# Differential heads: two pairs' norm products in one bank, posted behind the first scores

## The chip, the cores and the metric

The kernel runs on one core of a Trainium2 chip. The metric is device time in microseconds (us), the median of several runs. The core has a matrix engine (TensorE; PE in the profile, with its weight loads shown as PEld), a vector engine (DVE), a scalar engine (ACT), GpSimd (POOL), and a queue that issues the DMA transfers (SP). Products land in banks of PSUM, from which DVE and ACT read them; POOL works on SBUF only.

## The reference

A two-layer encoder over 1024 tokens of width 1024. Layer 0 has windowed, dense and memory cross attention; layer 1 has six differential heads and four cross-attention heads. Each layer ends in a gate, an output projection and the residual. What the change touches is layer 1's differential attention:

```python
def blk(args):                          # one block of 128 queries
    n, qi = args
    s = jnp.einsum("ibqhd,ibshd->ibhqs", qi, kk).astype(jnp.float32) * (D ** -0.5)
    ...
    p = jax.nn.softmax(s + rel_bias_lookup(table, rel)[None, None], axis=-1)
    w = p[0] - lam * p[1]
    return jnp.einsum("bhqs,bshe->bqhe", w.astype(v.dtype), v)
...
y_c = diff_attention_blocked(...)
y_c = rmsnorm(y_c, subln_g) * (1.0 - lam_init)
y = jnp.concatenate([y_c.reshape(Bn, S, -1), ...], axis=-1) * jax.nn.silu(gate)
return x + y @ w_out
```

The RMS norm of `y_c` runs over the 128 values that one head gives for one token. Its two small matrix products and what hangs on them are what moves.

## The kernel before, in words

**Steps.** Layer 1's attention is a list of 56 steps: 8 for cross attention, then 6 heads of 8 query blocks each, one block of 128 queries to a step. Two blocks (an even and an odd one) make a pair, and there are 24 pairs. `run_steps` (line 441) walks through the steps and posts, for step i, in this order: the DMA that copies the weights `e` of step i-1 (`hop`); the scores of step i (`s1`); some of the pending projection work (`jobs.pull`); whatever earlier pairs have left in `posts`; for the pair whose second block lies three steps back, the product with the values (`s3`, whose list of follow-up functions goes to `posts`); the transposes of the step two back (`s2`); the rest of step i's softmax (`finish`); and some more projection work.

**One differential step.** `s1` (line 1420) makes eight score matmuls: four with the high part of the keys (line 1433) and four with the low part (line 1439), which use 64 rows of the array each. I call the last four the kl scores. DVE adds the bias and takes the minimum (line 1445), ACT exponentiates (line 1448), DVE combines the two maps (line 1457). The result is copied by DMA and transposed two steps later, in eight transposes of 128x128 (line 540, tile `te`), four to a bank; ACT and DVE split each bank into a high and a low part (lines 315 and 316).

**One pair.** In the even step, `s3` multiplies the values by the transposed weights, 24 matmuls (line 1472, tile `oc`). ACT copies the result to `O` and squares it to `sq`. The norm follows in two posts. `d1`, in the step after: two products of `sq` with a column of ones (line 1487, tile `ssqc`; the profile shows each as two matmuls), ACT adds the epsilon term (line 1491, tile `z`), and POOL takes the power (line 229, tile `rz`). `d2`, one step later again: two transposes that spread the result over the partitions (line 1500, tile `rbcc`), DVE scales `O` (line 1502), POOL multiplies it into the gate tile (line 1505), and behind the last pair of a head the tile is stored (`store_y`).

**Banks.** `ps_t` (line 218) hands out banks of tag T, of which there are two. In layer 1's heads `te` takes two of them a step, `ssqc` and `rbcc` one each, and the transposes of the values (`tv`, line 405) one for each half of a head's values.

**Projection work.** `jobs.pull(n)` posts n groups of eight matmuls of 128x512 (line 297), which project the next heads' queries, keys, values and gates. In a differential step two groups come behind the scores and one at the end. When all projections are done, early parts of the output product (line 662, tile `pre`) come from the same place, one group behind the scores.

**Order.** The program's order gives each instruction its rank. The tool that builds the kernel plans the order on each engine from the ranks, from estimated durations and from the free buffers, so instructions of one engine can change places where a bank or an input is not there in the plan. `tc.issue_after` ties a few of them to another instruction.

Of the kernel before, what the change touches and what calls it, by code (L numbers as in the profile page):

```python
# [14 lines left out]
AF = mybir.ActivationFunctionType  # L15
# [3 lines left out]
P = 128  # L19
# [136 lines left out]
def encoder_kernel(ctx, tc, A):  # L156
    nc = tc.nc
# [23 lines left out]
    ones2 = const.tile([P, 2], F32, name="ones2")  # L181
# [36 lines left out]
    def ps_t(name):  # L218
        return ps.tile([P, 512], F32, tag="T", name=name, bufs=2)

    def ps_a(name):
        return ps.tile([P, 512], F32, tag="A", name=name, bufs=2)

    def stat(name, n=1, bufs=3):
        return sm.tile([P, n], F32, tag=name, name=name, bufs=bufs)

    def rstd_from(dst, var, n):
        nh = nhalf[:, :n] if isinstance(n, int) else nhalf[:, :n[0] * n[1]].rearrange("p (a b) -> p a b", b=n[1])
        return nc.gpsimd.tensor_tensor(out=dst, in0=var, in1=nh, op=ALU.pow)  # L229
# [83 lines left out]
    def split_to(hi, lo, src, scale=None):  # L313
        if scale is None:
            nc.scalar.copy(hi, src)  # L315
            return nc.vector.tensor_tensor(out=lo, in0=src, in1=hi, op=ALU.subtract)  # L316
        else:
            nc.scalar.activation(hi, src, AF.Identity, scale=scale)  # L318
            return nc.vector.scalar_tensor_tensor(out=lo, in0=src, scalar=scale, in1=hi,
                                           op0=ALU.mult, op1=ALU.subtract)  # L320
# [17 lines left out]
    def transpose_tile(xt, hT, t):  # L338
        hh, hl = hT
        for j in range(2):  # L340
            T = ps_t("tx")
            for i in range(4):
                k = 4 * j + i
                nc.tensor.transpose(T[:, i * P:(i + 1) * P], xt[:, k * P:(k + 1) * P], ident)
            o = slice(t * P, (t + 1) * P)
            Tv = T.rearrange("p (k c) -> p k c", k=4)
            split_to(hh[:, 4 * j:4 * j + 4, o], hl[:, 4 * j:4 * j + 4, o], Tv)
# [50 lines left out]
    def v_consume(M, c0, n, acc, put):  # L398
# [3 lines left out]
        def d():  # L402
            T = ps_t("tv")
            for i in range(n // P):
                nc.tensor.transpose(T[:, i * P:(i + 1) * P], raw[:, i * P:(i + 1) * P], ident)
            put(c0 // P, n // P, T)
# [34 lines left out]
    def run_steps(steps, jobs, hooks=None, pace=None):  # L441
        n = len(steps)
        posts = deque()
        p2 = p3 = 0
        finish = None
        for i in range(n + LAG + 1):
            behind = None
            if jobs is not None:
                jobs.step = i
            if hooks:  # L450
                hooks(i)
            if 0 < i <= n and steps[i - 1].hop:
                steps[i - 1].hop()
            if i < n:
                if steps[i].need:
                    jobs.ensure(*steps[i].need)
                finish = steps[i].s1()
            f = steps[min(i, n - 1)].fill
            if jobs is not None:
                if half[0] and len(wout) >= 8 and jobs.projected():  # L460
                    f = pace(i)
                two = f > 1 and p3 < n and p3 + steps[p3].lag + 1 <= i and steps[p3].s3b is not None
                jobs.pull(f - f // 2 - two)
                if hooks:
                    hooks(-1)
            for q in list(posts):
                q.pop(0)()
                if not q:
                    posts.remove(q)
            if p3 < n and p3 + steps[p3].lag + 1 <= i:  # L470
                st, p3 = steps[p3], p3 + 1
                if st.s3 is not None:
                    if st.need3:
                        jobs.ensure(*st.need3)
                    r = st.s3()
                    if r:
                        posts.append(r)
                    if st.s3b is not None:
                        jobs.pull(two)
                        st.s3b()  # L480
            if p2 < n and p2 + steps[p2].lag <= i:
                behind = steps[p2].s2()
                p2 += 1
            if finish:
                with (tc.issue_after(behind.ins) if behind is not None else nullcontext()):
                    finish()
                finish = None
            if jobs is not None:
                jobs.pull(f // 2)
                if hooks:  # L490
                    hooks(-1)
        while posts:
            for q in list(posts):
                q.pop(0)()
                if not q:
                    posts.remove(q)
# [170 lines left out]
    def store_y(l, m, g):  # L667
        dma(ysc[l][m], g)
        stored.add((l, m))
# [304 lines left out]
    for k in range(KT):  # L974
        if k % 2 == 0:
            T = ps_t("tm")
# [232 lines left out]
    def hooks0(i):  # L1209
        if 2 <= i < 8:  # L1210
            skew(i - 2)
        if i < 0:
            wout_hook(0, jobs, "g2", r1)

    run_steps(steps, jobs, hooks0, lambda i: i % 4 != 3)
    jobs.drain()
    top_stack.close()
# [176 lines left out]
    jobs = Jobs(jl, ld)  # L1394

    toeps = {}

    def load_toep(h):
        t = M.pl.tile([P, TOEP], F32, tag="toep", name="toep", bufs=2)
        dma(t[:, 768:1152], skew_src(h))  # L1400
        for i in range(2):
            nc.gpsimd.tensor_copy(t[:, 1152 * i:1152 * i + 768], far[:, i, h:h + 1].to_broadcast([P, 768]))
        toeps[h] = t
# [6 lines left out]
    for h in range(6):  # L1410
        for qb in range(8):
# [52 lines left out]
            if st.sub == 1:  # L1464
                def s3(h=h, qb=qb, grp=grp):
                    ph, pl_ = grp["pt"]
                    V = C[h]["v"]
                    acc = ps_a("oc")[:, :256]
                    n = 0
                    for kt in range(8):  # L1470
                        for v, pt in ((0, ph), (0, pl_), (1, ph)):
                            nc.tensor.matmul(acc, V[:, kt, v, :], pt[:, kt, :], start=(n == 0), stop=(n == 23))  # L1472
                            n += 1
                    O = M.pl.tile([P, 256], F32, tag="O", name="O", bufs=2)
                    nc.scalar.copy(O, acc)
                    sq = M.pl.tile([P, 256], F32, tag="sq", name="sqc", bufs=2)
                    nc.scalar.activation(sq, acc, AF.Square)
                    z2 = stat("es", 2)
                    zv = grp["z"].rearrange("p (t m) -> p t m", m=2)[:, :, 0]
                    nc.vector.scalar_tensor_tensor(out=z2, in0=zv, scalar=EPS, in1=zv,  # L1480
                                                   op0=ALU.mult, op1=ALU.mult)
                    st_ = {}

                    def d1():
                        T = ps_t("ssqc")
                        for i in range(2):
                            nc.tensor.matmul(T[:, 2 * i:2 * i + 2], sq[:, i * P:(i + 1) * P], ones2,  # L1487
                                             start=True, stop=True)
                        v = stat("z2", 2)
                        for i in range(2):  # L1490
                            nc.scalar.activation(v[:, i:i + 1], T[:, 2 * i:2 * i + 1], AF.Identity,
                                                 scale=1.0 / 128, bias=z2[:, i:i + 1])
                        r = stat("rz2", 2)
                        rstd_from(r, v, 2)
                        st_["r"] = r

                    def d2():
                        T = ps_t("rbcc")
                        for i in range(2):
                            nc.tensor.transpose(T[:, i * P:(i + 1) * P],  # L1500
                                                st_["r"][:, i:i + 1].to_broadcast([P, P]), ident)
                        nc.vector.scalar_tensor_tensor(out=O, in0=O, scalar=gs, in1=T[:, 0:256],  # L1502
                                                       op0=ALU.mult, op1=ALU.mult)
                        g = gates[h][:, (qb - 1) * P:(qb + 1) * P]
                        nc.gpsimd.tensor_tensor(out=g, in0=O, in1=g, op=ALU.mult)
                        if qb == 7:
                            store_y(1, 2 + h, gates[h])
                    return [d1, d2]
                st.s3 = s3
                st.need3 = ("v%d" % h, "g%d" % h)  # L1510
            st.need = ("k%d" % h, "q%d" % h)
            steps.append(st)
    def hooks1(i):
        if i == 3:
            load_toep(0)
        if i < 0:
            wout_hook(1, jobs, "g5", r2)

    run_steps(steps, jobs, hooks1, lambda i: 2)
    jobs.drain()  # L1520
    left.close()
# [74 lines left out]
```

## Time and profile before

| | |
|---|---|
| Runs | 1242.15, 1242.44, 1243.17 us; median 1242.44 |
| The profiled execution | 1241.79 us; its span, first to last instruction, 1240.0 us |
| Granted TensorE clock, mean | 0.997 |
| Layer 1's differential steps | from about 715 to 1175 us |
| `ssqc` matmuls | 96, from 733.2 to 1170.7 us |
| `rbcc` transposes | 48, from 741.7 to 1172.4 us |

All times in the profile are of one execution, counted from its first instruction. "Busy" is the time in which an engine had an instruction in work. TensorE's matmuls are pipelined, so a recorded length covers more than the time until the next can start; what a group costs is read from start to start. "Idle before" in square brackets names the time for which an engine stood still ahead of an instruction, and what released it.

### The profile page before, as it was taken

How to read it: one execution, taken by the hardware profiler on the slowest of the kernel's cores; microseconds unless marked ns; L12 is line 12 of the kernel's file. 1: busy time of each engine (PE TensorE's matmuls, PEld its weight loads, DVE VectorE, ACT ScalarE, POOL GpSimd, SP SyncE). 2: the span in 40 equal slices, each digit the busy share in tenths (PEclk: the TensorE clock that was granted, in tenths of full speed). 3: DMA queues.
4: the chain of work that ended last, by engine and by line, in shares of the span. 5: the costliest groups of instructions: out<-in, count | busy, mean ns of one | idle time of the engine just before them, and what ended most of it. 6: DMA issues, size and time to landing. Idle time of an engine off the chain costs nothing. (4 is left out here: it accounts for less than half of the span.)

```text
span 1240.0 us, 19680 instructions
## 1 busy us (share of the span) xinstructions
PE 1202.2 (97%) x6806; PEld 999.9 (81%) x6806; DVE 805.7 (65%) x1479; ACT 651.9 (53%) x1453; POOL 412.1 (33%) x390
## 2 busy tenths in 40 slices
PE   5999999999999899999999999999999999999997
PEld 4788888888887788877888788888787878877886
DVE  5547665477777778647356866766767676678544
ACT  6248754367667776533157633544444454456322
POOL 5023365466666655403022221222222121223100
PEclk9999999999999999999999999999999999999999
DMA  6664445545465565376545333242342432546354
GB/s 255 195 194 146 161 170 167 164 159 202 175 229 203 193 236 198 149 211 224 170 151 162 119 111 123 88 143 102 111 134 79 139 112 102 162 141 203 119 197 147
DMA packets 96638, 199.91 MB, mean 161 GB/s; under 512 B 11510, under 2 KB 31222, under 8 KB 96540
## 3 DMA queue, kind: packets, MB, share of 16 engines
q1 hardware_dynamic: 96540, 198.66, 47.7%
q8 instruction: 54, 0.88, 0.3%
q14 instruction: 44, 0.36, 0.1%
HBM read 79.32 MB, written 31.47 MB: 89 GB/s over the span
## 5 line engine op out<-in xcount | busy, mean ns | idle before, releaser
L297 PE MATMUL acc<-h,wh 128*128 128x512 f32 x1536 | 499.2, 398 | 2.1 <-DVE wh L239 0.8
L297 PEld LDWEIGHTS acc<-h,wh 128*128 128x128 f32 x1536 | 283.1, 188 | 66.9 <-issue 12.4
L297 PE MATMUL acc<-h,wl 128*128 128x512 f32 x768 | 304.5, 396 | 1.0 <-POOL wl L241 1.0
L241 POOL TENSOR_TENSOR wl<-wr,wh 128x512 fp32r<-128x512 f32 x96 | 124.4, 1296 | 334.5 <-DVE wh L239 147.2
L316 DVE TENSOR_TENSOR PTl<-te,PTh 128x512 fp32r<-128x512 f32 x224 | 148.3, 686 | 120.9 <-ACT PTh L315 118.3
L1448 ACT ACTIVATE e<-e,mn 128x1024 f32<-128x1024 f32 x96 | 110.1, 1149 | 126.2 <-DVE mn L1445 126.1
L297 PEld LDWEIGHTS acc<-h,wl 128*128 128x128 f32 x768 | 144.5, 188 | 34.0 <-issue 4.7
L315 ACT CAST PTh<-te 128x512 fp32r<-128x512 f32 x224 | 125.0, 590 | 18.3 <-PE te L540 15.2
L1445 DVE CUSTOM_DVE_ANT_0 e<-sc,toep 128x1024 f32<-128x1024 f32 x96 | 114.0, 1216 | 5.8 <-PE sc L1439 5.6
L1070 POOL TENSOR_TENSOR e<-e,rz 128x1024 f32<-128x1024 f32 x48 | 92.5, 1931 | 74.3 <-DVE rz L1069 56.6
L540 PEld LDWEIGHTS te<-identr,er 128*128 128x128 f32 x896 | 92.2, 143 | 18.1 <-issue 3.2
L540 PE MATMUL te<-identr,er 128*128 128x128 f32 x896 | 99.2, 246 | 5.3 <-issue 2.5
L239 DVE CAST wh<-wr 128x512 fp32r<-128x512 f32 x112 | 56.3, 504 | 42.1 <-PE acc L297 17.8
L1457 DVE SCALAR_TENSOR_TENSOR e<-e,mr 128x1024 f32<-128x1024 f32 x48 | 76.3, 1589 | 1.3
L1472 PE MATMUL oc<-PTh,v 128*128 128x256 f32 x384 | 74.8, 288 | 0.3 <-DVE ckl L1341 0.3
L662 PE MATMUL po<-woh,yl 128*128 128x512 f32 (+1 forms) x172 | 65.6, 382 | 0.0
L662 PE MATMUL po<-woh,yh 128*128 128x512 f32 (+1 forms) x172 | 65.6, 381 | 0.0
L662 PE MATMUL po<-wol,yh 128*128 128x512 f32 (+1 forms) x172 | 65.4, 380 | 0.0
L1061 DVE TENSOR_REDUCE mn<-sb 128x1 f32<-128x1024 f32 x48 | 58.4, 1216 | 7.2 <-PE sb L509 6.8
L1472 PEld LDWEIGHTS oc<-PTh,v 128*128 128x128 f32 x384 | 61.4, 191 | 0.6 <-DVE ckl L1341 0.5
L1066 ACT ACTIVATE e<-sb,mr,nrq 128x1024 f32<-128x1024 f32 x48 | 58.0, 1208 | 1.9
L318 ACT ACTIVATE yh<-yr 128x256 fp32r<-128x256 f32 (+2 forms) x56 | 23.9, 447 | 64.1 <-DMA yr<-ysc 30.2
(199 smaller groups left out, 2248.4 us busy)
## 6 DMA issues: line engine op xcount, KB each, us to landing
er<-e SPq DMA_DIRECT2D x112, 512.0 KB, 3.0
wr<-in_w_in SPq DMA_DIRECT2D x96, 256.0 KB, 2.7
ysc<-gy SPq DMA_DIRECT2D x16, 512.0 KB, 2.6
wor<-in_w_out SPq DMA_DIRECT2D x32, 256.0 KB, 3.4
cq<-sg SPq DMA_DIRECT2D x64, 128.0 KB, 2.5
ck<-sg SPq DMA_DIRECT2D x48, 128.0 KB, 2.3
er<-e SPq DMA_DIRECT2D x12, 384.5 KB, 2.9
xpsc<-xh SPq DMA_DIRECT2D x18, 256.0 KB, 2.4
```

The costliest lines, as they stand in the source:

```text
L241: (nc.vector if fast else nc.gpsimd).tensor_tensor(out=lo, in0=raw, in1=hi, op=ALU.subtract)
L297: lastmm[0] = nc.tensor.matmul(acc, a, b[:, k, c0:c0 + n], start=(i == 0), stop=(i == 23))
L315: nc.scalar.copy(hi, src)
L316: return nc.vector.tensor_tensor(out=lo, in0=src, in1=hi, op=ALU.subtract)
L540: nc.tensor.transpose(to[:, i * P:(i + 1) * P], e[0][:, k * P:(k + 1) * P], idt)
L662: lastmm[0] = nc.tensor.matmul(acc, a, b, start=(start and n == 0), stop=(stop and n == 2))
L1061: nc.vector.tensor_reduce(out=mn, in_=Sp, op=ALU.min, axis=AX.X)
L1070: nc.gpsimd.tensor_tensor(out=et, in0=et, in1=rz.to_broadcast([P, 1024]), op=ALU.mult)
L1445: nc.vector.tensor_tensor_reduce(out=et, in0=Sp, in1=toeps[h][:, w0:w0 + 1024], scale=1.0, scalar=BIG, op0=ALU.add, op1=ALU.min, accum_out ...
L1448: nc.scalar.activation(et, et, AF.Exp, bias=mn[:, m:m + 1], scale=-1.0, accum_out=z[:, m:m + 1])
L1457: nc.vector.scalar_tensor_tensor(out=es[0], in0=es[1], scalar=c, in1=es[0], op0=ALU.mult, op1=ALU.add)
L1472: nc.tensor.matmul(acc, V[:, kt, v, :], pt[:, kt, :], start=(n == 0), stop=(n == 23))
```

## The change

Three things are changed in the program.

1. In `run_steps` the loop over `posts` stands ahead of the first `jobs.pull` instead of behind it. Only the differential heads leave posts, so only they are touched.
2. `d1` of a pair now takes one bank for two things: the two transposes of the pair before (`turn`, columns 0 to 255) and its own products with ones (columns 256 to 259). Behind the power it posts the previous pair's scale, gate product and, where due, the store (`scale`). Transposes, scale and product of a pair therefore come one step later than before, in an odd step, and even steps have no post left.
3. The last pair of the last head has nobody behind it, and keeps a `d2` with a bank of its own.

```diff
@@ run_steps
                 finish = steps[i].s1()
             f = steps[min(i, n - 1)].fill
+            for q in list(posts):
+                q.pop(0)()
+                if not q:
+                    posts.remove(q)
             if jobs is not None:
...
                 jobs.pull(f - f // 2 - two)
                 if hooks:
                     hooks(-1)
-            for q in list(posts):
-                q.pop(0)()
-                if not q:
-                    posts.remove(q)
             if p3 < n and p3 + steps[p3].lag + 1 <= i:
@@ differential heads
+    spread = []
...
                     def d1():
                         T = ps_t("ssqc")
+                        late = spread.pop() if spread else None
+                        if late is not None:
+                            late[0](T)
                         for i in range(2):
-                            nc.tensor.matmul(T[:, 2 * i:2 * i + 2], sq[:, i * P:(i + 1) * P], ones2,
+                            nc.tensor.matmul(T[:, 256 + 2 * i:258 + 2 * i], sq[:, i * P:(i + 1) * P], ones2,
                                              start=True, stop=True)
                         v = stat("z2", 2)
                         for i in range(2):
-                            nc.scalar.activation(v[:, i:i + 1], T[:, 2 * i:2 * i + 1], AF.Identity,
+                            nc.scalar.activation(v[:, i:i + 1], T[:, 256 + 2 * i:257 + 2 * i], AF.Identity,
                                                  scale=1.0 / 128, bias=z2[:, i:i + 1])
                         r = stat("rz2", 2)
                         rstd_from(r, v, 2)
                         st_["r"] = r
-
-                    def d2():
-                        T = ps_t("rbcc")
+                        if late is not None:
+                            late[1](T)
+                        spread.append((turn, scale))
+
+                    def turn(T):
                         for i in range(2):
                             nc.tensor.transpose(T[:, i * P:(i + 1) * P],
                                                 st_["r"][:, i:i + 1].to_broadcast([P, P]), ident)
+
+                    def scale(T):
                         nc.vector.scalar_tensor_tensor(out=O, in0=O, scalar=gs, in1=T[:, 0:256],
                                                        op0=ALU.mult, op1=ALU.mult)
                         g = gates[h][:, (qb - 1) * P:(qb + 1) * P]
                         nc.gpsimd.tensor_tensor(out=g, in0=O, in1=g, op=ALU.mult)
                         if qb == 7:
                             store_y(1, 2 + h, gates[h])
-                    return [d1, d2]
+
+                    def d2():
+                        T = ps_t("rbcc")
+                        for f in spread.pop():
+                            f(T)
+                    return [d1, d2] if (h, qb) == (5, 7) else [d1]
```

## The prediction

> **What bounds the kernel now.** I read the page first, then busy time by stage, then TensorE's waits inside the differential heads, then its timeline through one pair of steps.
>
> ```profile
> PE 1202.2 (97%) x6806; PEld 999.9 (81%) x6806; DVE 805.7 (65%) x1479; ACT 651.9 (53%) x1453; POOL 412.1 (33%) x390
> ```
> ```profile
> 800.00:900.00 100.00, 100.00 (x565) 80.61 (x562) 69.74 (x121) 46.76 (x92) 22.20 (x23) 1.00 0.36 119
> 1000.00:1100.00 100.00, 100.00 (x567) 80.56 (x563) 67.07 (x120) 48.65 (x96) 18.73 (x19) 1.00 0.33 111
> 1100.00:1175.00 75.00, 72.46 (x429) 59.48 (x428) 54.41 (x94) 40.96 (x88) 19.05 (x18) 1.00 0.50 169
> ```
> ```profile
> PE te L540 <- ACT z L1491: 0.9, 1, 0.9
> PE te L540 <- DVE O L1502: 0.8, 1, 0.8
> PE rbcc L1500 <- POOL rz L229: 0.5, 1, 0.5
> ```
>
> The columns of the second fence are length, then busy time of PE, PEld, DVE, ACT and POOL, the granted clock, DMA share and rate. TensorE is busy for the whole of the heads' stage (100.00 of 100.00 us at clock 1.00) and DVE for 70. A small product that waits for nobody there can save nothing by starting earlier; only what it costs TensorE to go from one kind of matmul to the next, and the few real waits, can change. The only waits of 0.5 us or more from 715 to 1175 us are the three above.
>
> The prices lie in the timeline of one pair of steps (start, length as recorded, line, count). Recorded lengths overlap, so I subtract starts.
>
> ```profile
> 870.78 0.73 PE L1439 MATMUL sc<-ckl,cq 64*128 64x512 f32 x4
> 871.45 0.73 PE L297 MATMUL acc<-h,wh 128*128 128x512 f32 x2
> 872.01 0.39 PE L297 MATMUL acc<-h,wl 128*128 128x512 f32 x1
> ...
> 874.99 0.39 PE L297 MATMUL acc<-h,wh 128*128 128x512 f32 x1
> 875.22 0.50 PE L1487 MATMUL ssqc<-ones,sqc 128*128 128x2 f32 x4
> 875.58 0.51 PE L540 MATMUL te<-identr,er 128*128 128x128 f32 x4
> 875.92 0.47 PE L297 MATMUL acc<-h,wh 128*128 128x512 f32 x1
> 876.23 0.39 PE L297 MATMUL acc<-h,wl 128*128 128x512 f32 x1
> 876.46 0.45 PE L540 MATMUL te<-identr,er 128*128 128x128 f32 x4
> 876.75 0.70 PE L297 MATMUL acc<-h,wh 128*128 128x512 f32 x2
> ...
> 878.21 1.07 PE L1433 MATMUL sc<-ck,cq 128*128 128x512 f32 x4
> 879.21 0.73 PE L1439 MATMUL sc<-ckl,cq 64*128 64x512 f32 x4
> ...
> 883.64 0.38 PE L1500 MATMUL rbcc<-ident,rz 128*128 128x128 f32 x2
> 883.78 0.36 PE L1472 MATMUL oc<-PTh,v 128*128 128x256 f32 x1
> ...
> 886.74 0.81 PE L540 MATMUL te<-identr,er 128*128 128x128 f32 x8
> ```
>
> In the odd step the eight transposes of te come as four, two projection matmuls, four. The code posts them together, so the order on the engine is planned, and a bank that is not free yet is gone around. The bank is the one that ssqc took: T has two. In the even step (886.74) the eight come in one piece. I counted 24 such odd steps, one for each pair.
>
> Steady projection costs 0.229 us a matmul: 13 of them from 872.01 to 874.99.
>
> **What each boundary costs now, per pair.**
> - kl scores to projection: the first two matmuls take 872.01 - 871.45 = 0.56, against 0.458: 0.10.
> - ssqc itself: 875.58 - 875.22 = 0.36.
> - ssqc into te: four transposes take 0.34, against 0.29 behind a projection (876.75 - 876.46): 0.05.
> - The split of te: two projections take 876.46 - 875.92 = 0.54, against 0.458: 0.08 for going back into projection once more.
> - rbcc itself: 883.78 - 883.64 = 0.14.
> - rbcc into the 24 matmuls of oc: they take 886.74 - 883.78 = 2.96. The first pair has none ahead of it:
>
> ```profile
> 722.34 0.28 PE L1472 MATMUL oc<-PTh,v 128*128 128x256 f32 x1
> ...
> 725.21 0.81 PE L540 MATMUL te<-identr,er 128*128 128x128 f32 x8
> ```
>
> There it is 2.87, so 0.09. Together 0.82 us a pair.
>
> **What the pair costs afterwards.** In an odd step the previous pair's two transposes (turn) and this pair's ssqc stand directly behind the kl scores and ahead of 16 projection matmuls. Nothing small is left in an even step. Turn and ssqc keep their 0.14 and 0.36. Unknown are three entries. Kl scores into a small float32 product: the trace has one other case, the transposes of v.
>
> ```profile
> 779.10 0.73 PE L1439 MATMUL sc<-ckl,cq 64*128 64x512 f32 x3
> 779.76 0.66 PE L405 MATMUL tv<-ident,vraw 128*128 128x128 f32 x4
> 780.34 0.50 PE L1439 MATMUL sc<-ckl,cq 64*128 64x512 f32 x1
> ...
> 1089.36 0.60 PE L405 MATMUL tv<-ident,vraw 128*128 128x128 f32 x4
> 1089.72 1.18 PE L1433 MATMUL sc<-ck,cq 128*128 128x512 f32 x4
> 1090.83 0.73 PE L1439 MATMUL sc<-ckl,cq 64*128 64x512 f32 x4
> ```
>
> Within the kl scores four of them take 0.58, behind a projection 0.36: 0.22 more, but that includes going back to kl scores. So 0 to 0.22; I take 0.10, the price of the projection behind the kl scores, which has the same two neighbours in kind. Turn into ssqc: 0 to 0.09, the dearest such exit above; I take 0.05, ssqc into te. Ssqc into projection: 0.05 to 0.11 (the upper end: four L1433 take 1.11 us behind tv, 1089.72 to 1090.83, against 1.00 behind a projection, 878.21 to 879.21); I take 0.08, te into projection.
>
> Sum 0.14 + 0.36 + 0.10 + 0.05 + 0.08 = 0.73; a pair gains 0.09. By the ends it is 0.55 to 0.92, a gain of 0.27 or a loss of 0.10. For 23 pairs (the last keeps its own d2): 2.1 us gained, between 6.2 gained and 2.3 lost.
>
> ```profile
> 871.44 0.30 PEld L297 LDWEIGHTS acc<-h,wh 128*128 128x128 f32 x2 [0.36 <-issue]
> 871.79 0.19 PEld L297 LDWEIGHTS acc<-h,wl 128*128 128x128 f32 x1
> ```
>
> The first row is why the kl scores are an expensive neighbour: the weight loader stands idle for 0.36 us and loads only when they end. A load is recorded with 0.19; if all of it lay open at the entry of turn and at that of the projection behind ssqc, the pair would cost 0.14 + 0.36 + 0.19 + 0.05 + 0.19 = 0.93 and lose 0.11, 2.5 us in all. The Trainium skill (TensorE: Matmul & The Clock Gate, Step-by-step: what each phase is for) has the rule for it: a weight load is pulled ahead of running matmuls only if the row groups don't conflict or it goes into the background buffer; this speaks against the new place, and by it the sum would be near that loss. The row agrees that nothing is pulled ahead; but projection pays only 0.10 there, about half a load, and that is why I keep 0.10 and let the loss stand as a rival.
>
> **The bank.** The scale on DVE now holds the shared bank, and the question is whether the second half of te still meets it.
>
> ```profile
> 873.27 1.22 DVE L1445 CUSTOM_DVE_ANT_0 e<-sc,toep 128x1024 f32<-128x1024 f32 x1
> ...
> 874.41 0.08 DVE L1445 DVE_READ_ACCUMULATOR2_ANT mn<- 128x1 f32 x1
> ...
> 884.13 0.48 DVE L1502 SCALAR_TENSOR_TENSOR O<-O,misc,rbcc 128x256 f32<-128x256 f32 x1
> ```
>
> The kl scores end at 871.45 and the second score pass at 874.41. The scale takes 0.48 and stands behind both passes: bank free 3.45 us after the scores. The second half of te wants it after 0.73 of small products, 16 x 0.229, 0.08 and 0.29: 4.8 us. Margin 1.3, so te stays whole. Near the end the heads pull 8 matmuls instead of 16, te is there at 2.9 us, and about four splits stay: 0.3 us back. The boundaries give 1.8.
>
> **The waits.**
>
> ```profile
> 1115.72 0.50 PE L1487 MATMUL ssqc<-ones,sqc 128*128 128x2 f32 x4
> ...
> 1115.94 1.16 ACT L1448 ACTIVATE e<-e,mn 128x1024 f32<-128x1024 f32 x1 [2.35 <-DVE mn L1445]
> ...
> 1118.71 0.40 ACT L1491 ACTIVATE z<-ssqc,es 128x1 f32<-128x1 f32 x2
> ```
>
> The 0.9 us (te behind z, odd step) arises because ssqc, at 1115.72, is just too late: ACT takes up two exponentials first and reaches z at 1118.71. With ssqc 16 matmuls (3.7 us) earlier, z's 0.40 fall into the 2.35 us in which ACT waited for DVE; next late is the scale, which by the 3.45 is in time. The 0.8 us (te behind O on DVE, even step) goes because even steps take no small bank any more. Together 1.7 gained, or nothing if the scale brings an equal wait into odd steps. The 0.5 us before the last rbcc stays: the last d2 still waits for POOL's power.
>
> What else moves is covered. POOL's power for the new pair moves 3.7 us up with z, and nobody needs it for two steps. Each scale, gate product and store_y comes one step later, on DVE, POOL and SP; y's are read back only by the output products, and O has two buffers, used two steps apart each. The ssqc waits for the square on ACT, which stands in the step before, and 8 projections and the scores lie between. If that cover went, all of TensorE's queue would wait behind it. No new load is issued.
>
> Sum against the profiled execution, 1241.79 (span 1240.0): 1241.79 - 1.8 - 1.7 = 1238.3. The median of the runs, 1242.44, lies 0.65 above it; so 1238.9.
>
> **The rivals.**
> 1. The prices cancel. Small products behind the kl scores cost the 0.22 of tv or the whole open loads, a loss of 0.03 to 0.11 a pair (0.7 to 2.5), the four splits stay (0.3), and one of the two waits is gained (0.9): 1242.5 to 1244.3, 1242.9 as I weigh them. For it: the 0.36 above, and only one remote row for the first entry. Against it: the 0.22 has two transitions in it.
> 2. The order is planned, so the small products may land behind projections after all, as te was torn apart in every odd step. Then the splits and the waits stay and only the exit into oc is saved, 0.09 less 0.05 for turn into ssqc, 23 times: 0.9, 1241.5. Against it: turn's input is old by then and a bank is free.
> 3. Slower: the scale keeps the bank too long. DVE is 70% busy here; if another 1.3 us of its work, a product of e or a gate, is placed ahead of the scale, te meets the bank in each of some 20 odd steps. Every 0.1 us behind the 4.8 us costs 2 us; at 0.35 it is 7.0 lost against 3.5 gained: 1245.9. It decides where the scale ends later than 4.8 us behind the kl scores. For it: both late waits of today are just this kind. Against it: the margin, and that other matmuls can be planned into the gap at 0.08. The Trainium skill (PSUM — Partial Sum Buffer, PSUM bank collisions raise a hardware error) says that two engines may not be in one bank together, two readers included: by that the scale waits for both z's too. No row of before shows z and O on one bank.
>
> **How the numbers follow.** The forecast has 0.53, the cancelling 0.23, the planned order 0.12, the slower one 0.12. 0.2%, about what a measurement of this kernel can tell from no change, is 2.5 us: faster is below 1239.96. Of the forecast I leave 0.03 above that, as it rests on 2.1 us of small differences. Faster 0.50, within 0.38, slower 0.12. The range runs from 1235.8 (three quarters of the way from 2.1 to the 6.2 that the cheap ends allow, 3.1 us) to 1243.9 (every pair at its dear end, 2.3 lost, four splits, 0.3, and 1.1 of the 1.7 us of waits gained); it leaves out most of rival 3 and the tail below, 0.17 together. The forecast's own range is 1236 to 1240.4.
>
> **What would show it.** Right: in odd steps turn and ssqc between kl scores and projection, te in one piece of eight in about 20, oc in 2.87 us in even steps, no te wait on z or O. The three entries read directly off starts. Wrong: te still split in most steps, a te wait on DVE O in odd steps, first entries above 0.2, or a wait at ssqc on ACT's square.

## The result, and the profile after

| kernel | median, us | lowest to highest | runs |
|---|---|---|---|
| before | 1242.21 | 1240.54 to 1243.63 | 22 |
| changed | 1244.28 | 1241.02 to 1246.6 | 22 |

The ratio is 1.0015, with a 95% interval from 1.0009 to 1.0022: the change costs 1.1 to 2.7 us, where a gain of 3.5 was forecast and the range ended at 1243.9. The profiled execution took 1244.27 us, with a span of 1242.5 and a mean granted clock of 0.994.

First the page's line of busy times, then busy time by stage in the columns of before, then TensorE's waits from 715 to 1180 us.

```profile
PE 1201.3 (97%) x6806; PEld 1000.2 (81%) x6806; DVE 817.8 (66%) x1479; ACT 650.6 (52%) x1453; POOL 414.3 (33%) x390
```
```profile
800.00:900.00 100.00, 100.00 (x567) 80.94 (x568) 72.77 (x121) 46.43 (x92) 23.25 (x23) 1.00 0.37 120
1000.00:1100.00 100.00, 100.00 (x568) 81.14 (x567) 70.17 (x121) 49.06 (x97) 19.53 (x19) 1.00 0.34 112
1100.00:1175.00 75.00, 69.53 (x410) 57.03 (x409) 54.99 (x92) 40.28 (x87) 17.11 (x17) 0.98 0.50 167
```
```profile
PE pre L662 <- ACT sqc L1478: 3.1, 1, 3.1
PE te L540 <- DVE O L1511: 1.3, 1, 1.3
PE rbcc L1507 <- POOL rz L229: 0.5, 1, 0.5
PE tv L405 <- DVE PTl L316: 0.5, 1, 0.5
```

TensorE has the same 6806 matmuls and is as full as before up to 1100 us. In the stage from 1100 to 1175 its busy time falls from 72.46 to 69.53 us and the clock from 1.00 to 0.98. There stands a new wait of 3.1 us of the output product (`pre`) on ACT's square, which before did not have.

One odd step of the changed kernel on TensorE (start, length, line, count):

```profile
889.71 0.73 PE L1440 MATMUL sc<-ckl,cq 64*128 64x512 f32 x4
890.37 0.43 PE L1507 MATMUL ssqc<-ident,rz 128*128 128x128 f32 x2
890.64 0.51 PE L1492 MATMUL ssqc<-ones,sqc 128*128 128x2 f32 x4
891.01 0.71 PE L297 MATMUL acc<-h,wh 128*128 128x512 f32 x2
...
894.76 0.80 PE L540 MATMUL te<-identr,er 128*128 128x128 f32 x8
895.39 0.46 PE L297 MATMUL acc<-h,wh 128*128 128x512 f32 x1
```

This is the forecast picture: two transposes (0.27) and the ssqc products (0.37) directly behind the kl scores, 16 projections in 3.75, and te in one piece of eight.

**Where it is gained and where it is lost.** I place three marks: the first score matmul of the heads, that of step 49, and the end of the span.

```profile
680.35 0.70 PE L1434 MATMUL sc<-ck,cq 128*128 128x512 f32 x2
...
1087.81 1.18 PE L1434 MATMUL sc<-ck,cq 128*128 128x512 f32 x4
```

| profiled execution | heads start | to step 49 | from there to the end |
|---|---|---|---|
| before | 678.99 | 410.73 | 150.28 |
| changed | 680.35 | 407.46 | 154.69 |

The heads gain 3.27 us up to step 49 and lose 4.41 behind it, 1.1 in all. The spans of the two profiled executions differ by 2.5, because the heads of the second started 1.36 us later; that lies ahead of everything that the change touches, and in the profiles of this study, with the same program up to there, the start varies from 677.3 to 680.7.

**The late chain.** DVE, POOL and TensorE at steps 51 and 52 of the changed kernel:

```profile
1109.33 1.31 DVE L1456 SCALAR_TENSOR_TENSOR mr<-mn,misc,rz 128x1 f32<-128x1 f32 x1
1110.68 2.32 DVE L1458 SCALAR_TENSOR_TENSOR e<-e,mr 128x1024 f32<-128x1024 f32 x1
...
1113.53 1.21 DVE L1446 CUSTOM_DVE_ANT_0 e<-sc,toep 128x1024 f32<-128x1024 f32 x1
...
1115.81 0.47 DVE L1511 SCALAR_TENSOR_TENSOR O<-O,misc,ssqc 128x256 f32<-128x256 f32 x1
```
```profile
1108.10 3.83 POOL L258 TENSOR_TENSOR wol<-wor,woh 128x512 fp32r<-128x512 f32 x3 [10.19 <-ACT woh L257]
```
```profile
1114.55 0.45 PE L540 MATMUL te<-identr,er 128*128 128x128 f32 x4
1116.34 0.54 PE L540 MATMUL te<-identr,er 128*128 128x128 f32 x4 [1.33 <-DVE O L1511]
...
1126.07 0.39 PE L662 MATMUL pre<-woh,yl 128*128 128x512 f32 x1
1129.59 0.79 PE L662 MATMUL pre<-woh,yh 128*128 128x512 f32 x1 [3.13 <-ACT sqc L1478]
1130.19 0.63 PE L662 MATMUL pre<-wol,yh 128*128 128x512 f32 x1
1130.61 0.63 PE L662 MATMUL pre<-woh,yl 128*128 128x512 f32 x1
```

From 1000 to 1090 us, mr (one column) takes 0.218 us and e 1.63 on average, in both kernels. Here they take 1.31 and 2.32, beside three splits of the output weights on POOL (3.83 for three, 1.28 each). The second split ends at 1108.10 + 2.55 = 1110.65, and so does mr (1110.64); the third ends at 1111.93, and e follows 1.07 later. So the score passes, the scale behind them, and then te's bank are late, and te waits 1.33. The same happens once more at 1120.70, in step 52 (mr 1.25, e 2.29). Such holds are not new: in before, mr and e take 0.96 and 2.28 in step 51, and 0.21 and 2.31 in step 52. Then the passes of step 52, ACT's two exponentials and its square come so late that TensorE, which has arrived with `pre`, stands for 3.13 us. Behind that wait its clock is halved, as these windows show (the column ahead of the last two is the granted clock):

```profile
1128.00:1130.00 2.00, 0.41 (x1) 0.41 (x2) 0.37 (x1) 2.00 (x6) 1.22 (x1) 0.80 0.96 346
1130.00:1132.00 2.00, 2.00 (x6) 1.52 (x6) 1.95 (x5) 1.54 (x4) 0.00 (x0) 0.50 0.78 200
1132.00:1134.00 2.00, 2.00 (x10) 1.23 (x8) 1.93 (x3) 0.00 (x0) 0.00 (x0) 0.85 0.52 161
```

Matmuls of `pre` follow each other at 0.42 (1130.19 to 1130.61) instead of 0.23.

**Theory after this.** The early posts gain what the forecast said. The shared bank makes te hang on a scale that stands behind DVE's score passes; near the end DVE has no slack, because POOL's splits hold it, and the delay comes out as a stop of TensorE and a lower clock. Rivals: the shared bank costs a little in every pair; the loss comes from the output product's accumulators, which change in step 52; DVE simply has too much work. The section on why the prediction was wrong says what became of this theory.

### The profile page after: what moved, and what is told of

Same layout as the page of the kernel before. It is cut to its first block, busy times and chain, and to the rows that moved or that the text cites. A ratio compares the mean times of both kernels' runs of the same rounds, so it can differ in the third digit from the quotient of the medians.

```text
span 1242.5 us, 19649 instructions
## 1 busy us (share of the span) xinstructions
PE 1201.3 (97%) x6806; PEld 1000.2 (81%) x6806; DVE 817.8 (66%) x1479; ACT 650.6 (52%) x1453; POOL 414.3 (33%) x390
## 4 chain that ended last, share of the span: by engine, by line
PE 51%; DVE 1%; issue 1%; ACT 0%; DMA 0%; SPq 0%; POOL 0%; POOLq 0%; DVEq 0%; ACTq 0%
PE acc L297 25%; PE po L662 6%; PE oc L1473 5%; PE sc L1434 4%; PE sc L1440 3%; PE te L540 3%; PE pre L662 2%; PE ssqc L1492 1%; PE ox L616 1%; PE ssqc L1507 1%; PE sx L509 1%; PE tv L405 1%; DVE xs L1303 0%; DVE e L1446 0%; PE tx L344 0%
## 5 line engine op out<-in xcount | busy, mean ns | idle before, releaser
L229 POOL TENSOR_TENSOR rz<-z,nhalf 128x2 f32<-128x2 f32 x24 | 17.7, 737 | 271.4 <-ACT z L1496 254.5
L540 PEld LDWEIGHTS te<-identr,er 128*128 128x128 f32 x896 | 89.1, 141 | 16.6 <-issue 3.5
L540 PE MATMUL te<-identr,er 128*128 128x128 f32 x896 | 95.0, 244 | 4.5 <-issue 2.5
L239 DVE CAST wh<-wr 128x512 fp32r<-128x512 f32 x112 | 59.3, 531 | 41.4 <-PE acc L297 19.2
```

The costliest lines, as they stand in the source:

```text
L239: nc.vector.tensor_copy(hi, raw)
L540: nc.tensor.transpose(to[:, i * P:(i + 1) * P], e[0][:, k * P:(k + 1) * P], idt)
```

## The experiments

All were timed against before on the same chip. "Shared" means the changed kernel's bank for two pairs, "own" the banks of before. I tell them by question. Each profile shows one execution, and its time need not be near the median: it is 1240.96 us for the early posts alone, 1244.99 for the shared bank alone, 1248.63 with the posts ahead of the scores and 1235.78 for the changed kernel without splits, where the medians are 1238.14, 1242.25, 1246.29 and 1239.31. Waits read from those four are of that execution.

### Which part of the change costs

**The early posts alone** (before, with the loop over `posts` moved, banks as before).

```diff
             f = steps[min(i, n - 1)].fill
+            for q in list(posts):
+                q.pop(0)()
...
-            for q in list(posts):
-                q.pop(0)()
```

> Only the loop over the posts is moved; ssqc and rbcc keep a bank each. Theory (one wait near the end of the heads made the change slower: the first product of a new output group waits behind oc for its bank, 3.13 us in the profile after, and the clock falls to 0.50 behind it): even steps still take a small bank, so the second half of te waits for DVE's scale of O as before (about 0.8 to 1.3 us) and the output group then waits less than 3 us; the heads before that gain 1 to 2 us by te coming in one piece. Time 1241 to 1243. Rival (small products behind the kl scores are dear in every pair): 1244 to 1245, as after.

Measured 1238.14 us, ratio 0.9969 (0.9958 to 0.9981): faster than before and than the changed kernel, and better than expected. It reaches step 49 407.78 us after its first scores, 2.95 earlier than before did, so the gain in the regular steps is that of the early posts; the shared bank adds 0.3. Te is in one piece in every step. From step 49 it needs 150.99, where the changed kernel needs 154.69 and before 150.28. It waits for the square too, but in two short pieces (and 1.0 us for a `yl` on DVE), and the clock from 1120 to 1140 stays 1.00:

```profile
PE pre L662 <- ACT sqc L1477: 1.6, 2, 1.2
```

**The shared bank alone** (changed, with the loop at its old place).

> Only the shared bank; the posts stand behind the projections as before. Theory (the wait near the end): even steps take no small bank, te comes in one piece behind oc and the new output group is reached before oc's bank is free, so the wait of about 3 us and the fall of the clock are there: 1244 to 1245.5, no better than after. Rival (the dear place behind the kl scores): it is gone here, 1241 to 1242.5.

Measured 1242.25, ratio 0.9996 (0.9987 to 1.0006). The time is the rival's. But its profile has the late wait (2.0 us on the square) and the clock of 0.91 from 1120 to 1140, as the theory had it; up to step 49 it is 1.9 us ahead, and that is given back.

### Where the wait sits

**One more group of `pre` in step 52** (changed), so that no accumulator begins there.

```diff
-    run_steps(steps, jobs, hooks1, lambda i: 2)
+    run_steps(steps, jobs, hooks1, lambda i: 3 if i == 52 else 2)
```

> The changed kernel with one number changed: at step 52 the heads pull two groups of the early output product ahead of oc instead of one, so that the accumulator changes ahead of oc and not right behind it. Theory (the wait near the end): the 3.13 us wait on ACT's square and the 1.6 us of half clock behind it go, 1239 to 1240.5, faster than both. Rival (dear place in every pair, or chance in layer 0): 1244 as after.

Measured 1243.2, ratio 1.0006 (0.9998 to 1.0015). A miss: the wait did not go, it moved to the product with the values. The profile puts it down to a cast of output weights on ACT that stands between step 52's two late exponentials (1126.65 and 1128.31).

```profile
PE oc L1473 <- ACT woh L257: 3.2, 1, 3.2
```

So the change of accumulator is not what makes the wait. It fits that whatever on TensorE needs the late chain first has to wait; why oc needs that cast, the trace does not show.

**Twelve useless matmuls in step 52** (changed; they write a score bank that nobody reads).

```diff
+        if i == 152:
+            junk = ps_s("junk")
+            for _ in range(12):
+                nc.tensor.matmul(junk[:, 0:512], C[5][(0, 1)][:, 0:P], C[5]["k"][0][:, 0:512],
+                                 start=True, stop=True)
```

> The changed kernel with 12 useless matmuls of 128x512 into a free score bank behind the transposes of step 52; they fill about 2.75 us of the wait and nobody reads them. If the clock falls because TensorE stands still for 3 us, it stays up: granted clock 1.00 from 1125 to 1135 us, the eight output products behind take 1.9 us instead of 3.5, 1242 to 1243 although more work is done. If the clock has another cause: 1244 to 1245. If the wait isn't where I think, the 2.75 us come on top: 1247.

Measured 1242.94, ratio 1.0006 (0.9997 to 1.0014). The clock stays at 1.00, and the wait on the square is filled:

```profile
1120.00:1140.00 20.00, 18.93 (x105) 14.83 (x105) 16.46 (x28) 10.02 (x21) 4.58 (x5) 1.00 0.67 222
```

That ties the fall of the clock to the stop; the 12 matmuls take 2.9 us instead (1124.73 to 1127.62), and its other wait, te for the scale, grew to 2.6 us in two pieces.

**Own banks in the last part** (changed up to step 49, then as with the early posts alone).

```diff
-                        late = spread.pop() if spread else None
+                        late = spread.pop() if spread and (h, qb) <= (4, 5) else None
...
-                    return [d1, d2] if (h, qb) == (5, 7) else [d1]
+                    return [d1, d2] if (h, qb) >= (4, 5) else [d1]
```

> The changed kernel, except that from the pair of head 4, blocks 4 and 5, on each pair keeps its two transposes and its scale in a post and a bank of its own, as in the kernel with the early posts alone (1238.14). Up to step 49 it is the changed kernel. Theory (the shared bank loses its 4 us only near the end, where the vector engine is full): the time is that of the early posts alone, 1237.5 to 1239.5, no wait of TensorE on the square above 1.5 us, clock 1.00 from 1100 to 1140. Rival A (the shared bank costs a little in each pair, all through the heads): 1242 to 1243.5. Rival B (the loss comes from the planning of the output product's accumulators and not from the bank): 1242 to 1244.5, with the 3 us wait as before.

Measured 1238.69, ratio 0.997 (0.9959 to 0.9981). The theory's number; no wait on the square above 0.3 us, clock 1.00. So the shared bank costs its time in the last pairs. DVE and POOL at the place shown above, in this kernel:

```profile
1109.12 0.22 DVE L1456 SCALAR_TENSOR_TENSOR mr<-mn,misc,rz 128x1 f32<-128x1 f32 x1
1109.37 1.28 DVE L1458 SCALAR_TENSOR_TENSOR e<-e,mr 128x1024 f32<-128x1024 f32 x1
...
1111.18 1.22 DVE L1446 CUSTOM_DVE_ANT_0 e<-sc,toep 128x1024 f32<-128x1024 f32 x1
```
```profile
1107.88 1.29 POOL L258 TENSOR_TENSOR wol<-wor,woh 128x512 fp32r<-128x512 f32 x1 [3.82 <-ACT woh L257]
1109.43 3.65 POOL L258 TENSOR_TENSOR wol<-wor,woh 128x512 fp32r<-128x512 f32 x2 [0.26 <-ACT woh L257]
```

Here mr falls into a gap of 0.26 us between two splits and e starts before the next one; now it is POOL that is stretched (3.65 for two splits), and the passes start at 1111.18 instead of 1113.53. Whoever starts first holds the other.

**Two banks, same place** (changed, but the earlier pair's transposes get a bank of their own).

```diff
                         if late is not None:
-                            late[0](T)
+                            R = ps_t("rbcc")
+                            late[0](R)
```

> The changed kernel, except that the previous pair's two transposes take a bank of their own; their place in the odd step and that of the scale and gate product stay. The bank for the second half of the next transposes is still freed by the scale. Theory (what costs is that the scale and with it the bank come in the odd step, late behind the score passes, not that two products lie in one bank): like the changed kernel, 1242.5 to 1245, with a wait of about 1 us for the scale in a late odd step. Rival (two engines in one bank cost the time): 1238 to 1240.

Measured 1247.95, ratio 1.0044 (1.0032 to 1.0056), slower than expected by 3. The rival's time did not come, but the run does not decide between the two: with a bank apart for each, the small products themselves wait 3.0 us in a late odd step, tag T having two banks, and the wait on the square is there as well (2.3).

```profile
PE ssqc L1493 <- DVE v L316: 3.0, 1, 3.0
```

**Posts ahead of the scores** (changed, loop moved above `s1`, so that the scale precedes the passes on DVE).

> The changed kernel, with the posts one place earlier still: ahead of the step's scores, so that the scale stands ahead of the two score passes on the vector engine and the shared bank is free before the transposes need it. Theory (the bank is late because the scale stands behind the passes): no wait of TensorE for the scale; the splits of GpSimd still meet the vector engine, so some of the wait on the square may stay: 1238 to 1241.5. Rival (the loss is the splits' alone, the scale's place does nothing): 1242 to 1244.5.

Measured 1246.29, ratio 1.0035 (1.0021 to 1.0048): a miss for both. No wait for the scale is left, but that on the square is still 2.8 us, scores wait 1.3, and mr and e still take 0.92 and 1.94 on average from 1100 to 1135. In step 52 they take 1.25 and 2.28. The scale's place on DVE alone is not the cause.

### What POOL's splits do

**Without them.** The low parts of every second weight block are not computed: the high part is copied in their place by DMA. Once in the changed kernel, once with the early posts alone.

```diff
+        if l == 1 and i % 2:
+            dma(lo, hi)
+        else:
             (nc.gpsimd if i % 2 else nc.vector).tensor_tensor(out=lo, in0=raw, in1=hi, op=ALU.subtract)
```

> The changed kernel, with the low parts of every second block of layer 1's output weights copied from the high part by DMA instead of computed on GpSimd, so that part of the computation is left out and GpSimd has 16 splits of 1.3 us less. Theory (vector instructions are stretched while GpSimd works on a split, the score passes and the square on ACT come late, TensorE waits 3 us and loses its clock): the wait on the square falls below 1.5 us, the clock from 1100 to 1140 is 0.98 or more, 1238.5 to 1241. Rival (the scale in the odd step alone makes the delay): the wait stays at 2 to 3 us, 1242.5 to 1244.5.

> The kernel with the early posts alone (1238.14), with the same copy by DMA in place of the 16 splits on GpSimd (the low parts of the odd blocks of layer 1's output weights are left out), as the control for the run before. Theory: little is to be gained here, as the splits meet no late chain: 1236.5 to 1238.5, 0 to 1.5 us less. Rival (the splits on GpSimd cost the same in every kernel, whatever the place of the scale): 3 to 5 us less, 1233 to 1235.

Measured 1239.31, ratio 0.9979 (0.9964 to 0.9994), and 1238.23, ratio 0.9967 (0.9955 to 0.9979). Without the splits the changed kernel is 4.5 us faster (1.0015 to 0.9979) and the other gains nothing that can be told, as the theory had it. Mr and e are back at 0.22 and 1.28, the wait on the square falls to 1.1.

**In quarters.** Each split in four instructions of 128 columns (changed).

```diff
+            for j in range(0, 512, 128):
+                nc.gpsimd.tensor_tensor(out=lo[:, j:j + 128], in0=raw[:, j:j + 128], in1=hi[:, j:j + 128],
+                                        op=ALU.subtract)
```

> The changed kernel, with each of GpSimd's 16 splits of layer 1's output weights made in four instructions of 128 columns instead of one of 512. The same work on GpSimd, in shorter pieces. Theory (a vector instruction that meets a split is held until that one GpSimd instruction ends, up to 1.3 us each): the small product mr and the combination e are held by 0.4 us at most, so the score passes of the steps at 1110 and 1120 start 1 to 2 us earlier, the wait on the square falls to 0.5 to 2 us, and the time is 1239 to 1241.5. Rival (the two share a throughput, whatever the pieces): mr and e take as long as before, 1242.5 to 1245.

Measured 1241.04, ratio 0.9991 (0.9982 to 1.0): within the theory's range. POOL pays for it (6.07 us for three splits instead of 3.83), yet DVE is held for the length of a short instruction only:

```profile
1109.23 0.48 DVE L1461 SCALAR_TENSOR_TENSOR mr<-mn,misc,rz 128x1 f32<-128x1 f32 x1
1109.75 1.45 DVE L1463 SCALAR_TENSOR_TENSOR e<-e,mr 128x1024 f32<-128x1024 f32 x1
...
1111.72 1.21 DVE L1451 CUSTOM_DVE_ANT_0 e<-sc,toep 128x1024 f32<-128x1024 f32 x1
```
```profile
1107.98 6.07 POOL L260 TENSOR_TENSOR wol<-wor,woh 128x128 fp32r<-128x128 f32 x12 [9.13 <-ACT woh L257]
```

The Trainium skill (SBUF — State Buffer, Who interferes with whom) has the rule for it: a DVE instruction with two SBUF inputs and a GpSimd instruction that reads SBUF exclude each other for the whole instruction, and the one that starts first holds the pair. The rows agree: mr ends where a split ends, 1.31 us beside splits of 1.28 and 0.48 beside quarters. For e they agree but for about 0.2 us: it ended 1.07 behind the split that held it, where it takes 1.28 alone.

**All splits on DVE**, again in both kernels.

```diff
-        (nc.gpsimd if i % 2 else nc.vector).tensor_tensor(out=lo, in0=raw, in1=hi, op=ALU.subtract)
+        (nc.gpsimd if l == 0 and i % 2 else nc.vector).tensor_tensor(out=lo, in0=raw, in1=hi, op=ALU.subtract)
```

> The changed kernel, with all splits of layer 1's output weights on the vector engine, none on GpSimd: 16 instructions of 0.68 us more there, 10.9 us, about half of them between 1100 and 1140. Theory (the held instructions cost more than the work): mr back at 0.2 us and e at 1.3 us, 1238.5 to 1242. Rival (the vector engine is simply full, and any more work on it comes out at the end): a wait on the square above 3 us, 1244 to 1249. The planned order on TensorE differs from about 1125 on, so this is the weaker test of the two.

> The kernel with the early posts alone (1238.14), with all splits of layer 1's output weights on the vector engine. Theory (here no late chain meets the splits, so 10.9 us more work on the vector engine bring nothing and may cost): 1238 to 1241. Rival (GpSimd's splits hold the vector engine everywhere): faster, 1235 to 1237.

Measured 1237.74, ratio 0.9966 (0.9953 to 0.998), and 1235.99, ratio 0.9949 (0.9936 to 0.9963). DVE gets work and the kernels get faster, which speaks against the rival of a DVE that merely has too much to do; in the changed kernel the planned order on TensorE changes with it, as the expectation says. The changed kernel's groups from 1100 to 1135 us, with the mean in ns behind the bar, and the second kernel's last stage:

```profile
L258 DVE TENSOR_TENSOR wol<-wor,woh 128x512 fp32r<-128x512 f32 x13 | 9.1, 727 | 3.1 <-ACT woh L257 3.1
L1458 DVE SCALAR_TENSOR_TENSOR e<-e,mr 128x1024 f32<-128x1024 f32 x3 | 3.8, 1280 | 0.0
L1456 DVE SCALAR_TENSOR_TENSOR mr<-mn,misc,rz 128x1 f32<-128x1 f32 x3 | 0.6, 212 | 0.0
```
```profile
1100.00:1175.00 75.00, 74.47 (x438) 61.61 (x437) 52.65 (x97) 38.73 (x86) 9.00 (x11) 1.00 0.56 187
```

For the second I had expected 1238 to 1241 and hit the rival's 1235 to 1237. The splits do hold DVE there too (mr 1.32 and e 2.29 in step 51 of the kernel with splits on POOL), though the intervals of the two, 0.9958 to 0.9981 and 0.9936 to 0.9963, still overlap. It is the fastest kernel of the study, 6 us below before, with TensorE busy for 74.47 of 75 us. Against this stands that the copy by DMA gained nothing in that kernel; why, the runs don't settle (it adds transfers).

The ratios in one table:

| | splits on POOL | copied by DMA | all on DVE |
|---|---|---|---|
| own banks, early posts | 0.9969 | 0.9967 | 0.9949 |
| shared bank, early posts (the change) | 1.0015 | 0.9979 | 0.9966 |

The shared bank costs 0.46% (5.7 us) beside POOL's splits and 0.12 to 0.17% without them, which the intervals don't tell from nothing.

## Why the prediction was wrong, point by point

- **What bounds the kernel.** Right up to 1100 us. For the stage behind it the row that I quoted had DVE at 54.41 of 75 us; that mean hid stretches in which it has no slack.
- **Boundaries.** Right. Entry and transposes 0.27 against 0.24 forecast, entry and ssqc 0.37 against 0.41, 16 projections 3.75 against 3.74; te takes 0.63 against 0.58. Oc follows in 2.88 against 2.87. Gained up to step 49: 3.27 us, where 2.1 was forecast for boundaries in all 23 pairs. Part of the surplus is a wait of 0.30 on `ckl` in the first pair, which has gone.
- **That the shared bank is needed for it.** Wrong without being said: the kernel with own banks gains 2.95 there by the early posts alone. Small products behind kl scores cost there 0.47 and 0.19, those of the shared bank 0.27 + 0.37.
- **The bank.** Right in regular steps, exactly: the scale ends 3.45 us behind the kl scores (893.82 against 890.37, row below), and te is split four and four in three late steps only (1114.55, 1136.69 and 1153.48 us), where about four were forecast.

```profile
893.35 0.47 DVE L1511 SCALAR_TENSOR_TENSOR O<-O,misc,ssqc 128x256 f32<-128x256 f32 x1
```

- **The waits: "next late is the scale, which by the 3.45 is in time".** This step failed, but it has the smaller part of the loss. The 3.45 was taken from one regular step at 870 us and carried to 1110, where the DVE instructions ahead of the passes are held by POOL's splits. There the scale ends 6.1 us behind the kl scores (1110.19 to 1116.28), and te waits 1.33. The two waits of before went, as forecast (0.9 and 0.8); in their place came 1.3 and 3.1, and 1.5 us of reduced clock: the eight matmuls of `pre` took 6.55 us, 3.42 without the wait, against 1.92 in the step before. I had allowed for "nothing if the scale brings an equal wait", not for more than that. The 1.33 is little in itself: the kernel with the early posts alone stands 1.04 at the same place for `yl`. Nor does it make the square late: step 52's reciprocal, ahead of mr on DVE, starts at 1119.55 here and at 1119.44 there, in executions whose heads start at 680.35 and 680.43.
- **Cover: "What else moves is covered".** This is the step that failed for the larger part: it put the later place of scale and gate product, and ACT's square, at nothing. Of the power it was true. The rows of POOL and DVE in the changed kernel, then with the early posts alone:

```profile
1116.36 0.85 POOL L1514 TENSOR_TENSOR gy<-O,gy 128x256 f32<-128x256 f32 x1 [2.80 <-DVE O L1511]
1119.21 3.98 POOL L258 TENSOR_TENSOR wol<-wor,woh 128x512 fp32r<-128x512 f32 x3 [2.00 <-ACT woh L257]
1120.70 1.25 DVE L1456 SCALAR_TENSOR_TENSOR mr<-mn,misc,rz 128x1 f32<-128x1 f32 x1
1121.99 2.29 DVE L1458 SCALAR_TENSOR_TENSOR e<-e,mr 128x1024 f32<-128x1024 f32 x1
```
```profile
1119.64 0.22 DVE L1455 SCALAR_TENSOR_TENSOR mr<-mn,misc,rz 128x1 f32<-128x1 f32 x1
1119.89 1.28 DVE L1457 SCALAR_TENSOR_TENSOR e<-e,mr 128x1024 f32<-128x1024 f32 x1
1124.87 0.74 POOL L1505 TENSOR_TENSOR gy<-O,gy 128x256 f32<-128x256 f32 x1 [11.35 <-PE oc L1472]
1125.56 4.69 POOL L258 TENSOR_TENSOR wol<-wor,woh 128x512 fp32r<-128x512 f32 x3
```

  In step 51 both kernels are held alike (mr 1.31 and 1.32), and their passes start at 1113.53 and 1113.49. Then they part. With the early posts alone, POOL's next splits come behind a gate product that waits for a scale of the even step 52; POOL stands still for 11.35 us, and mr and e pass free. In the changed kernel the gate product is done in the odd step, and the splits run beside step 52's mr and e. Its passes start at 1124.80 against 1122.03; of these 2.8 us, mr and e have 2.0. ACT's square starts at 1129.17 against 1126.93, and TensorE's wait at this place is 3.13 us against 1.16, so some 2 us of it are this lateness.

  Against before, whose heads started 1.36 us earlier, the square is not late. ACT in the changed kernel, then in before:

```profile
1129.17 0.37 ACT L1478 ACTIVATE sqc<-oc 128x256 f32<-128x256 f32 x1
```
```profile
1128.50 0.38 ACT L1477 ACTIVATE sqc<-oc 128x256 f32<-128x256 f32 x1
```

  Counted from the heads' first scores, oc ends 2.8 us earlier than in before (1125.14 against 1126.57 us) and the square starts 0.7 earlier. TensorE brought its gain to this place, and the chain over DVE and ACT did not follow; with the early posts alone its square is 3.0 earlier.
- **The rivals.** The third names a mechanism that did occur, a scale that holds the bank behind other DVE work, and its time, 1245.9, is nearer than my forecast. But it was to act in some 20 odd steps for 0.35 us each; it acted in one, for 1.33, and the larger part of the loss came as the wait on the square and the clock behind it. That its time is near is luck. The first had nearly the right time for a wrong reason: prices did not cancel.

**What stays open.** Whether mr meets a split depends on fractions of a us (a gap of 0.26 in one kernel). With the early posts alone mr is held as long on average, 0.92 from 1100 to 1135 us, but in steps 51 and 53 and not in 52, and that kernel loses little by it. So the runs show that the shared bank and the splits cost together what neither costs alone. That the gate product's place on POOL brings them together is read from the rows: the kernels with one more group of `pre`, with the useless matmuls, with two banks and with the posts ahead of the scores have the splits beside step 52's mr and e too (1.24 or 1.25, and 2.28), and the one with own banks in the last part has not (0.22 and 1.28). No run moves the gate product alone. Nor do the runs show that every arrangement with a shared bank must meet the splits this way.

## What to carry to other kernels

Check a margin that was measured in a regular step again in the stage where the last loads, splits and steps come together, since a bank held for a scale hangs on everything queued ahead of it there. When a product moves to another step, look at what it stood ahead of on its engine, for that may now start earlier and meet something else. When a change has two parts, price each alone: here one part had the whole gain and the other the whole loss. And before moving elementwise work to GpSimd, look at what DVE's instructions beside it take: 0.68 us of work on DVE was cheaper than 1.28 on POOL that held it.

## What the runs showed of the hardware

- A DVE instruction of one column took 0.22 us alone and up to 1.31 beside a GpSimd subtraction of 1.28, whose end it met; beside one cut into quarters, 0.48. In the other order GpSimd was stretched, two splits to 3.65 us.
- After a stop of 3.13 us the granted clock was 0.50 for two us and 0.85 in the two behind them. In the kernel with the shared bank alone a stop of 2.00 us was enough for 0.75 and then 0.50, two us each. A stop of 1.76 us (splits in quarters) and the one of 1.33 left no mark, and with 12 useless matmuls in the gap the clock stayed at 1.00.
